# An encoder layer on eight cores: attention steps at whole instead of half yields, exponentials issued as a pair, new rates and stage order, and earlier loads

## Chip, cores, metric

One Trainium2 chip, all 8 cores, each with two of the 16 sequences. The metric is the device time of the slowest core in microseconds (us). Some executions fall in a slower state, in which one die, sometimes both, shows a lower granted TensorE clock (in a run of before of 4717.97 us, 0.817 to 0.821 on one die and 0.985 to 0.987 on the other); only fast runs are compared, or, where a chip was often disturbed, the mean span of the four cores of dies whose clock stayed above 0.978. That second measure ("die mean" below) lies some 10 to 25 us under the mean of the slowest core.

## The reference, cut

```python
x = x + 0.5 * swiglu(rmsnorm(x), gate1, up1, down1)          # feed-forward 1
h = rmsnorm(x); q_A,k_A,v_A,q_B,k_B,v_B,g = split(h @ w_in)
o_A = differential_attention(q_A,k_A,v_A)   # dense, 8 heads x 2 maps, ALiBi, per-head norm
o_B = window_attention(q_B,k_B,v_B,sink)    # |t-s| <= 128, 16 query and 4 key heads
x = x + (sig(g0)*(o_A @ P_A) + sig(g1)*(o_B @ P_B)) @ w_out
x = x + 0.5 * swiglu(rmsnorm(x), gate2, up2, down2)          # feed-forward 2
return rmsnorm(x)
# x: (16, 2048, 1024) float32; d_ff 2816
```

## The kernel before

A builder in Python emits all instructions in one order; semaphores follow from it. Each core has 8 blocks of 512 tokens. Stages are GU (gate and up of a feed-forward), D (down), W (input projections), P (gates and the two attention projections), O (output projection). Attention is not a stage: its 328 steps per sequence are put in between the dense products of other stages, so that TensorE has dense work while ScalarE (ACT) makes exponentials and VectorE (DVE) multiplies by the ALiBi table. Where steps may go in is a "yield" of a stage.

```python
def gemm8(self, b, bk, w, wk, H, hk):           # one PSUM bank of dense products
    for kc in range(8):
        self.mm(b, w[:, kc, :], H[:, kc, :], kc == 0, kc == 7, ...)
        if kc == 3:
            yield "h"                           # a half yield: a step may go in here
...
def b_qk(...):                                  # scores of one step: two PSUM pairs
    ...
    def ex(s, et, ek, W, tab, tk):
        self.act(et, scores, AF.Exp, ...)       # ACT, 128 x 1024
        self.tt(et, et, tab, ALU.mult, ...)     # DVE
    ex(*post[0])
    self.part.append(lambda: ex(*post[1]))      # emitted only at the next yield
...
def dole(self, n):                              # hands out queued DMA issues
    if self.dq[0]: ...                          # attention's loads first, by SyncE
    elif self.dq[1] and n - self.doled >= (3 if self.ph2 else 5): ...   # the rest
...
DENSE = {"GU": 0.22, "D": 0.40, "W": 0.34, "P": 0.28, "O": 0.22}  # attention per dense work
```

In the later part, loads and stores of the second kind are issued by POOL (GpSimd), which also computes the reciprocal roots of the attention's per-head norm (`rs`) and of the RMS norms. Weights come as float32, are cast to bf16 by POOL's transfers on first use, and are then read from a bf16 copy in memory.

The softmax here doesn't subtract the row's maximum and nothing guards it: scores larger than these inputs give would overflow.

## Time and profile before

| | before |
|---|---|
| median of the first 4 runs | 4113.34 us (4105.45 to 4573.34, the highest one slow) |
| slowest core in the profile | 4117.7 us |
| TensorE busy | 3931.4 us, 95% |
| DVE, ACT, POOL busy | 57%, 45%, 6% |

An engine's line of the page gives busy us, share of the span and the number of instructions. A timeline line gives start, duration, engine, line, operation, output<-inputs, count, and in brackets the idle time before it with what ended it. L376 is the helper that emits every matrix product, so products are told apart by their tiles: `H,ra` are dense ones of GU and W (normalized block, weights), `aT,rd` those of D, `qD,kD` dense-attention scores, `vD,et` their value products, `qS,kS` and `vS,es` the windowed ones. Of the tiles that products wait for, `et`, `es` and `est` are exponentials, `fr` the first pass over a dense bank, `sq` and `ssv` copies of projections on their way to memory, `nh` and `rh` steps of a norm, `obs` and `otS` attention outputs, `ra` and `rd` weights.

### The profile page before, as it was taken

How to read it: one execution, taken by the hardware profiler on the slowest of the kernel's cores; microseconds unless marked ns; L12 is line 12 of the kernel's file. 1: busy time of each engine (PE TensorE's matmuls, PEld its weight loads, DVE VectorE, ACT ScalarE, POOL GpSimd, SP SyncE). 2: the span in 40 equal slices, each digit the busy share in tenths (PEclk: the TensorE clock that was granted, in tenths of full speed). 3: DMA queues.
4: the chain of work that ended last, by engine and by line, in shares of the span. 5: the costliest groups of instructions: out<-in, count | busy, mean ns of one | idle time of the engine just before them, and what ended most of it. 6: DMA issues, size and time to landing. Idle time of an engine off the chain costs nothing.

```text
span 4117.7 us, 76905 instructions; the slowest of 8 cores (4074.8 to 4117.7 us)
## 1 busy us (share of the span) xinstructions
PE 3931.4 (95%) x27236; PEld 2026.8 (49%) x27236; DVE 2351.7 (57%) x4564; ACT 1863.1 (45%) x2576; POOL 251.3 (6%) x362
## 2 busy tenths in 40 slices
PE   8999998999998899999988999999998999999998
PEld 3444455555555455555544555555554544444443
DVE  5445232567677567666455667767767654353533
ACT  3422022656566466556455656656655532021211
POOL 1010000000001000000000000000000000000000
PEclk8999999999999999999999999999999999999999
DMA  8867599865678767755744544544544356465544
GB/s 186 201 135 184 134 205 182 188 165 147 152 179 190 196 157 184 188 149 160 218 125 140 154 129 145 166 132 139 158 135 146 113 172 219 154 194 168 185 153 130
DMA packets 296259, 675.25 MB, mean 164 GB/s; under 512 B 31280, under 2 KB 145328, under 8 KB 295216
## 3 DMA queue, kind: packets, MB, share of 16 engines
q1 hardware_dynamic: 263440, 542.65, 44.4%
q0 software_dynamic: 31872, 126.63, 16.4%
q8 instruction: 230, 3.77, 0.4%
q14 instruction: 141, 1.16, 0.1%
q10 hardware_dynamic: 576, 1.05, 0.1%
HBM read 605.09 MB, written 160.79 MB: 186 GB/s over the span
## 4 chain that ended last, share of the span: by engine, by line
PE 85%; DVE 4%; DMA 3%; issue 3%; ACT 2%; SPq 1%; POOL 0%; DVEq 0%; ACTq 0%; POOLq 0%
PE bank L376 85%; SPq L404 1%; ACT et L379 1%; PE bank L1133 1%; DVE nacc L382 1%; DMA vS<-vs_d 1%; DMA rd<-s_d 1%; DMA qs_d<-sq 1%; DVE et L382 0%; DVE H L385 0%; DMA oTa<-od_d 0%; ACT fr L379 0%; POOL r L382 0%; DMA ra<-s_win 0%; DMA H<-h_d 0%
## 5 line engine op out<-in xcount | busy, mean ns | idle before, releaser
L376 PE MATMUL bank<-H,ra 128*128 128x512 bf16 x8320 | 1915.5, 383 | 42.5 <-DMA H<-h_d 20.0
L376 PEld LDWEIGHTS bank<-H,ra 128*128 128x128 bf16 x8320 | 785.8, 98 | 1098.3 <-issue 258.2
L379 ACT ACTIVATE et<-bank 128x1024 bf16<-128x1024 f32 x1024 | 1011.2, 1022 | 443.2 <-PE bank L376 439.3
L382 DVE TENSOR_TENSOR et<-et,td 128x1024 bf16<-128x1024 bf16 x1024 | 701.8, 688 | 471.8 <-ACT et L379 470.3
L376 PE MATMUL bank<-aT,rd 128*128 128x512 bf16 x2816 | 643.4, 381 | 2.6 <-DMA rd<-s_d 1.6
L385 DVE SCALAR_TENSOR_TENSOR fr<-fr,bank 128x512 f32<-128x512 f32 x480 | 329.3, 686 | 441.5 <-ACT fr L379 354.6
L376 PE MATMUL bank<-vD,et 128*128 128x129 bf16 x8192 | 554.1, 221 | 18.8 <-DVE obs L382 17.1
L376 PEld LDWEIGHTS bank<-vD,et 128*128 128x128 bf16 x8192 | 503.7, 98 | 117.7 <-issue 37.4
L379 ACT ACTIVATE fr<-bank 128x512 f32<-128x512 f32 x352 | 210.1, 597 | 668.8 <-PE bank L376 659.8
L376 PEld LDWEIGHTS bank<-aT,rd 128*128 128x128 bf16 x2816 | 261.4, 98 | 358.2 <-issue 74.2
L376 PE MATMUL bank<-qD,kD 64*128 64x512 bf16 x2048 | 322.4, 384 | 18.2 <-ACT et L379 14.6
L385 DVE SCALAR_TENSOR_TENSOR R<-bank,R 128x512 f32<-128x512 f32 x192 | 132.2, 688 | 266.3 <-PE bank L376 266.0
L382 DVE TENSOR_TENSOR aT<-fr,bank 128x512 bf16<-128x512 f32 x352 | 240.6, 684 | 60.8 <-PE bank L376 58.5
L379 ACT ACTIVATE es<-bank 128x768 bf16<-128x768 f32 (+1 forms) x256 | 191.3, 781 | 141.2 <-PE bank L376 141.1
L379 ACT ACTIVATE fr<-bank,bgh 128x512 f32<-128x512 f32 x128 | 88.0, 687 | 301.7 <-PE bank L376 300.2
L382 DVE TENSOR_TENSOR es<-es,sw 128x768 bf16<-128x768 bf16 (+1 forms) x256 | 137.5, 539 | 131.1 <-ACT es L379 126.1
L382 POOL TENSOR_TENSOR rs<-ms,mhalf 128x4 f32<-128x4 f32 x64 | 74.4, 1163 | 2118.9 <-DVE ms L385 2118.9
L382 DVE TENSOR_TENSOR nacc<-nacc,ntmp 128x512 f32<-128x512 f32 x224 | 154.0, 688 | 55.5 <-ACT ntmp L379 50.6
L379 ACT ACTIVATE sq<-bank 128x512 bf16<-128x512 f32 x104 | 62.1, 597 | 259.3 <-PE bank L376 199.6
L379 ACT ACTIVATE ntmp<-R 128x512 f32<-128x512 f32 x224 | 133.9, 628 | 98.3 <-DVE nacc L382 55.9
L376 PE MATMUL bank<-ra,H 128*128 128x256 bf16 x1280 | 155.1, 278 | 12.9 <-ACT sq L379 11.6
L376 PEld LDWEIGHTS bank<-ra,H 128*128 128x128 bf16 x1280 | 123.7, 100 | 47.7 <-issue 29.0
(103 smaller groups left out, 2222.7 us busy)
## 6 DMA issues: line engine op xcount, KB each, us to landing
ra<-s_gu SPq DMA_DIRECT2D x275, 512.0 KB, 4.0
rd<-s_d SPq DMA_DIRECT2D x200, 352.0 KB, 3.2
ra<-s_win SPq DMA_DIRECT2D x81, 512.0 KB, 6.5
ra<-s_pg SPq DMA_DIRECT2D x64, 512.0 KB, 4.2
ra<-s_pp SPq DMA_DIRECT2D x64, 512.0 KB, 3.5
ra<-w_gu POOLq DMA_DIRECT2D x33, 512.0 KB, 7.2
qD<-qd_d SPq DMA_DIRECT2D x128, 128.0 KB, 4.5
R<-x_d POOLq DMA_DIRECT2D x32, 512.0 KB, 8.4
```

The costliest lines, as they stand in the source:

```text
L376: self.S.add("pe", lambda e: e.matmul(out, lhsT=lhsT, rhs=rhs, start=start, stop=stop), r=r, w=w)
L379: self.S.add("act", lambda e: e.activation(out=out, in_=in_, func=func, **kw), r=r, w=w)
L382: self.S.add(eng, lambda e: e.tensor_tensor(out=out, in0=a, in1=b, op=op), r=r, w=w)
L385: self.S.add("dve", lambda e: e.scalar_tensor_tensor(out=out, in0=a, scalar=s, in1=b, op0=op0, op1=op1), r=r, w=w)
L404: self.S.add(eng, lambda e: e.dma_start(out=out, in_=in_), r=r, w=w, dma=sem)
L1133: self.S.add("pe", lambda e, q=q: e.transpose(out=bt[:, q * 128:(q + 1) * 128], in_=src[:, q, :], identity=self.ident), r=[sk, "ident"], w ...
```

## The change

Its intent, as far as the diff tells: keep TensorE from waiting. Parts: no half yields; both exponentials of a step at once, only the second multiply put off; other rates; blocks 4 and 5 share one W stage and norms move; odd projection weights are cast ahead; windowed values (vS) loaded in halves; loads handed out faster, in the last W stage by SyncE; one drain of background work less. In the code, `bulk` means that POOL issues the loads of the second kind.

```diff
     def gemm8(self, b, bk, w, wk, H, hk):
         for kc in range(8):
             self.mm(...)
-            if kc == 3:
-                yield "h"
...
+        self.casts = [("win", i) for i in WORDER if i % 2]
+                if k == "D" and bl == (2, 3) and n % 7 == 0:
+                    self.cast()
...
-        elif self.dq[1] and n - self.doled >= (3 if self.ph2 else 5):
+        elif self.dq[1] and n - self.doled >= (1 if self.ph2 else 3 if self.w7 else 5):
...
         def ex(s, et, ek, W, tab, tk):
             self.act(... AF.Exp ...)
+        def al(s, et, ek, W, tab, tk):
             self.tt(... ALU.mult ...)
         ex(*post[0])
-        self.part.append(lambda: ex(*post[1]))
+        al(*post[0])
+        ex(*post[1])
+        self.part.append(lambda: al(*post[1]))
...
-            if bt == 7 and u < 7 and u % 2:
-                self.load_vS(sq, (u + 1) // 2)
+            if bt in (4, 7) and u < 7 and u % 2:
+                self.load_vS(sq, (u + 1) // 2, int(bt == 7))
...
-              ("GU", (4,), 1), ("D", (4,), 1), ("GU", (5,), 1), ("D", (5,), 1), ("W", (4,), 1)]
-        for b in (6, 7):
-            st += [("GU", (b,), 1), ("D", (b,), 1), ("W", (b - 1,), 1)]
-        st += [("W", (7,), 1)]
+              ("GU", (4,), 1), ("D", (4,), 1), ("GU", (5,), 1), ("D", (5,), 1), ("W", (4, 5), 1),
+              ("GU", (6,), 1), ("D", (6,), 1), ("GU", (7,), 1), ("D", (7,), 1), ("W", (6,), 1), ("W", (7,), 1)]
...
-        span = [(at("W", (2, 3), 1) + 32, w7 + 12), (w7 + 22, at("P", (4,), 2) - 6)]
+        span = [(at("W", (2, 3), 1) + 32, w7 + 4), (w7 + 22, at("P", (4,), 2) - 6)]
+            self.w7 = k == "W" and bl == (7,)
+            self.bulk = (ph == 2 or bl[0] >= 4) and not self.w7
...
-    DENSE = {"GU": 0.22, "D": 0.40, "W": 0.34, "P": 0.28, "O": 0.22}
+    DENSE = {"GU": 0.25, "D": 0.33, "W": 0.30, "P": 0.28, "O": 0.25}
...
         if k == "GU":
-            self.drain()
+            if b != 3:
+                self.drain()
... (where norms are started in the first part: cut)
```

More of the change, by code (lines that the diff above doesn't have):

```diff
@@ L295, in decl_chip @@
             S.region(("kSb", k), *S.regions[("kS", k)][:1], 2048, ("kS", k))
-        self.vS = sb("vS", [128, 16, 65], BF16)
+        self.vS = sb("vS", [128, 16, 65], BF16, keys=([("vS", k) for k in range(2)], 1040))
         self.sw = sb("sw", [128, 2, 384], BF16)
@@ L429, in init_rings @@
         self.ncast = 0
-        self.casts = [t for c in range(8) for t in (("pg", c), ("pp", c))] + [("wo", i) for i in range(4)]
+        self.casts = [("win", i) for i in WORDER if i % 2]
+        self.casts += [t for c in range(8) for t in (("pg", c), ("pp", c))] + [("wo", i) for i in range(4)]
         self.casts += [("gu2", f) for f in range(22)] + [("d2", c) for c in range(16)]
@@ L682, in gu_tile @@
         bg, bgk = self.bank(True)
-        yield from self.gemm8(bg, bgk, w[:, 0], wk, H, ("H", hi))
+        self.gemm8(bg, bgk, w[:, 0], wk, H, ("H", hi))
         t, tk = self.frn()
@@ L689, in gu_tile @@
         bu, buk = self.bank(True)
-        yield from self.gemm8(bu, buk, w[:, 1], wk, H, ("H", hi))
+        self.gemm8(bu, buk, w[:, 1], wk, H, ("H", hi))
         self.tt(self.aT[ai][:, f, :], s, bu, ALU.mult, [sk, buk], [("aT", ai, f)])
@@ L746, in w_tile @@
                                 tt == 0 and kc == 0, tt == 1 and kc == 7, [wk, ("H", hi, kc)], [bk])
-                    if tt == 0:
-                        yield "h"
                 self.open = None
@@ L773, in w_tile @@
                 bb, bk = self.bank(True)
-                yield from self.gemm8(bb, bk, w[:, j], wk, H, ("H", hi))
+                self.gemm8(bb, bk, w[:, j], wk, H, ("H", hi))
                 self.copy(("act", "dve")[j], st[:, j, :], bb, [bk], [("sq", q, j)])
@@ L788, in w_tile, with st_W @@
         yield
-    def st_W(self, bl, his, tiles):
-        for i in tiles:
-            w, wk = self.take("a")
-            for b, hi in zip(bl, his):
-                yield from self.w_tile(i, w, wk, b, hi)
-            self.issue("a")
+    def st_W(self, bl, his, lead=1):
+        held = {}
+        n = len(bl)
+        order = [(i, f) for i in range(n) for f in range(lead)]
+        order += [(i, f) for f in range(lead, len(WORDER)) for i in range(n)]
+        for i, f in order:
+            if i == 0:
+                held[f] = self.take("a")
+            yield from self.w_tile(WORDER[f], *held[f], bl[i], his[i])
+            if i == n - 1:
+                self.issue("a")
     def st_P(self):
@@ L806, in st_P @@
                 bb, bk = self.bank(True)
-                yield from self.gemm8(bb, bk, wg[:, s], wgk, H, ("H", 1))
+                self.gemm8(bb, bk, wg[:, s], wgk, H, ("H", 1))
                 t, tk = self.frn()
@@ L812, in st_P @@
                 src, nm = ((self.oTa, "oTa"), (self.oTb, "oTb"))[s]
-                yield from self.gemm8(bb, bk, wp[:, s], wpk, src, (nm,))
+                self.gemm8(bb, bk, wp[:, s], wpk, src, (nm,))
                 m, mk = self.frn()
@@ L830, in st_O @@
                 bb, bk = self.bank(True)
-                yield from self.gemm8(bb, bk, w[:, j], wk, self.mT, ("mT",))
+                self.gemm8(bb, bk, w[:, j], wk, self.mT, ("mT",))
                 self.stt(self.R[ri][:, c, :], bb, 0.5, self.R[ri][:, c, :], ALU.mult, ALU.add,
@@ L881, in load_sw, with load_vS @@
         self.later_dma("sw", self.sw, self.sw_d[p].rearrange("p (a b) -> p a b", a=2), [("swd", p)], ["sw"], ("bsw", 0), q=0)
-    def load_vS(self, sq, g):
-        self.later_dma("vS", self.vS, self.vs_d[sq, g], [("vs", sq, b) for b in range(4 * sq, 4 * sq + 4)], ["vS"], ("bvs", 0), q=0)
+    def load_vS(self, sq, g, k):
+        self.later_dma(("vS", k), self.vS[:, 8 * k:8 * k + 8, :], self.vs_d[sq, g][:, 8 * k:8 * k + 8, :],
+                       [("vs", sq, b) for b in range(4 * sq + 2 * k, 4 * sq + 2 * k + 2)], [("vS", k)], ("bvs", k), q=0)
     def first_loads(self, sq, part):
@@ L899, in first_loads @@
             self.load_sw(0)
-            self.load_vS(sq, 0)
+            self.load_vS(sq, 0, 0)
+            self.load_vS(sq, 0, 1)
             self.load_qD(sq, 0, 1)
@@ L916, in attention @@
             self.second()
-            if not self.half:
-                self.turn(i)
+            self.turn(i)
             if sq == 0 and i % 5 == 3:
@@ L922, in attention @@
                 self.b_av(i, i - LAG, batches[i - LAG], sq)
-            if self.half:
-                self.turn(i)
             if i < n:
@@ L1047, in b_av @@
         else:
-            self.flush("vS")
+            self.flush(("vS", 0))
+            if bt >= 4:
+                self.flush(("vS", 1))
             ns = [0] if bt == 0 else [2 * bt - 1, 2 * bt]
@@ L1055, in b_av @@
                     self.mm(self.bk[bank][:, o:o + 65], self.es_[x % 4][:, c_, col:col + 128], self.vS[:, x, :],
-                            z == 0, z == len(mm) - 1, [("est", x % 4), "vS"], [("bk", bank)])
+                            z == 0, z == len(mm) - 1, [("est", x % 4), ("vS", x // 8)], [("bk", bank)])
                 self.evac_S(i, sq, u, ns, bank)
-            if bt == 7 and u < 7 and u % 2:
-                self.load_vS(sq, (u + 1) // 2)
+            if bt in (4, 7) and u < 7 and u % 2:
+                self.load_vS(sq, (u + 1) // 2, int(bt == 7))
     def evac_D(self, i, sq, u, qb):
@@ L1182, in build @@
         self.slot = -1
-        self.half = False
+        self.urgent = False
         self.dc = 0
@@ L1187, in build @@
         self.ph2 = False
+        self.w7 = False
         self.load_x(0, True)
@@ L1209, in build @@
         for q, (a, b) in enumerate(span):
-            marks[a - (16, 10)[q]] = lambda q=q: self.first_loads(q, 0)
-            marks[a - (8, 6)[q]] = lambda q=q: self.first_loads(q, 1)
+            marks[a - (16, 14)[q]] = lambda q=q: self.first_loads(q, 0)
+            marks[a - (8, 8)[q]] = lambda q=q: self.first_loads(q, 1)
         n, done = 0, 0
@@ L1214, in build @@
             self.ph2 = ph == 2
-            self.bulk = ph == 2 or len(bl) == 1
+            self.w7 = k == "W" and bl == (7,)
+            self.bulk = (ph == 2 or bl[0] >= 4) and not self.w7
             self.gset = [6, 7] if any(a <= n < b for a, b in span) else [6, 7, 0, 1, 2, 3, 4, 5]
             self.rate = 3 if n == 0 else 1
-            for y in self.begin(k, bl, ph):
-                self.half = y == "h"
-                if not self.half:
-                    n += 1
-                    if n == 9:
-                        self.rate = 1
-                    if n in (40, 46, 52, 58):
-                        self.issue("d")
-                    if n in marks:
-                        while self.bg2:
-                            self.step()
-                        marks[n]()
-                    self.second()
-                    self.fill()
+            for _ in self.begin(k, bl, ph):
+                n += 1
+                if n == 9:
+                    self.rate = 1
+                if n in (40, 46, 52, 58):
+                    self.issue("d")
+                if k == "D" and bl == (2, 3) and n % 7 == 0:
+                    self.cast()
+                if n in marks:
+                    while self.bg2:
+                        self.step()
+                    marks[n]()
+                self.second()
+                self.fill()
+                self.post()
+                if self.urgent:
@@ L1232, in build @@
                     self.post()
-                    if k == "W" and len(bl) == 1 and n % 2:
-                        self.post()
-                    self.dole(n)
-                pos = cum[n] + (cum[n + 1] - cum[n]) / 2 if self.half else cum[n]
+                self.dole(n)
                 want = 0
                 for q, (a, b) in enumerate(span):
-                    if n >= a and pos > cum[a]:
-                        want = total * q + int(total * min(1.0, (pos - cum[a]) / (cum[b] - cum[a])) + 1e-6)
+                    if n > a:
+                        want = total * q + int(total * min(1.0, (cum[n] - cum[a]) / (cum[b] - cum[a])) + 1e-6)
@@ L1241, in build @@
                     if n == a:
                         self.gset = [6, 7]
-                if self.half and self.mark == "pe":
-                    continue
-                if done < want or len(self.gset) > 2 and not self.half:
+                if done < want or len(self.gset) > 2:
                     self.pre()
@@ L1251, in build @@
                 for q, (a, b) in enumerate(span):
-                    if n == b and not self.half:
+                    if n == b:
                         assert done == total * (q + 1)
@@ L1271, in begin @@
         b = bl[0]
-        two = len(bl) == 2
-        if ph == 1:
-            if two:
-                if k == "GU":
-                    if b == 0:
-                        self.load_x(2)
-                        self.load_x(3)
-                        return self.st_GU((0, 1), 4)
-                    self.drain()
-                    for j in range(2):
-                        self.store_x1(j)
-                        self.bg.append(self.norm(j, 1, j, store=lambda j=j: self.after2(j, j)))
-                    return self.st_GU((2, 3))
-                self.drain()
-                if k == "D":
-                    if b == 0:
-                        for j in (2, 3):
-                            self.bg.append(self.norm(j, 0, j, need=("x", j)))
-                    return self.st_D(bl)
+        if k == "D":
+            self.dc = 0
+            self.free = True
@@ new lines, in begin @@
+        if ph == 1 and b < 4:
+            if k == "GU":
+                if b == 0:
+                    self.load_x(2)
+                    self.load_x(3)
+                    return self.st_GU((0, 1), 4)
+                self.drain()
+                for j in range(2):
+                    self.store_x1(j)
+                    self.bg.append(self.norm(j, 1, j, store=lambda j=j: self.after2(j, j)))
+                return self.st_GU((2, 3))
+            self.drain()
+            if k == "D":
@@ L1291, in begin @@
                 if b == 0:
                     for j in (2, 3):
-                        self.store_x1(j)
-                        self.bg.append(self.norm(j, 1, j, store=lambda j=j: self.store_h2(j, j)))
-                else:
-                    self.bg.append(self.norm(0, 0, 0, need=("x", 4)))
-                self.S.add("dve", lambda e: e.memset(self.ssv[1], 1.0), w=[("ssv", 1)])
-                return self.st_W(bl, bl, WORDER)
+                        self.bg.append(self.norm(j, 0, j, need=("x", j)))
@@ L1299, in begin @@
+                return self.st_D(bl)
+            self.S.add("dve", lambda e: e.memset(self.ssv[1], 1.0), w=[("ssv", 1)])
+            if b == 0:
+                for j in (2, 3):
+                    self.store_x1(j)
+                    self.bg.append(self.norm(j, 1, j, store=lambda j=j: self.store_h2(j, j)))
+            else:
+                self.bg.append(self.norm(0, 0, 0, need=("x", 4)))
+            return self.st_W(bl, bl)
+        if ph == 1:
             if k == "GU":
                 self.drain()
+                if b in (5, 7):
+                    self.mix(b - 1)
@@ L1301, in begin @@
                 return self.st_GU((0,))
             if k == "D":
-                if b == 4:
-                    self.bg.append(self.norm(1, 0, 0, need=("x", 5)))
-                if b == 5:
-                    self.mix(4)
+                if b in (4, 6):
+                    self.bg.append(self.norm(1, 0, 0, need=("x", b + 1)))
+                else:
+                    self.mix(b, lambda c: self.dc > c)
                 return self.st_D(bl)
-            self.drain()
-            if b < 7:
-                self.mix(b + 1)
@@ L1311, in begin @@
-            if b < 6:
-                self.bg.append(self.norm(b % 2, 0, 0, need=("x", b + 2)))
+            if b == 4:
+                self.store_x1(5)
+                self.urgent = True
+                self.bg.append(self.norm(0, 0, 0, need=("x", 6)))
+                return self.st_W(bl, (1, 2), 4)
+            if b == 6:
+                self.store_x1(7)
             if b == 7:
+                self.drain()
                 self.load_p(0, (0,))
-            return self.st_W(bl, (self.MIX[b],), WORDER)
+            return self.st_W(bl, (self.MIX[b],))
@@ L1324, in begin @@
         if k == "GU":
-            self.drain()
+            if b != 3:
+                self.drain()
             if b == 2:
@@ L1333, in begin @@
             return self.st_GU((0,) if b < 7 else (1,))
-        self.dc = 0
-        self.free = True
         if b == 7:
@@ L1356, in end, with mix @@
                 self.bg.append(self.normf(5))
-    def mix(self, b):
-        self.store_x1(b)
-        self.bg.append(self.norm(b % 2, 1, self.MIX[b], store=lambda: self.after2(b, self.MIX[b])))
+    def mix(self, b, ready=None):
+        if ready is None:
+            self.store_x1(b)
+        self.bg.append(self.norm(b % 2, 1, self.MIX[b], store=lambda: self.after2(b, self.MIX[b]), ready=ready))
     def after2(self, b, hi):
         self.store_h2(b, hi)
+        self.urgent = False
         if b < 2:
```

## The prediction

> **What bounds the kernel now.** I read the busy shares first, then the stretches by stage, then TensorE's idle times one by one, and last the queues that ended them. The page and the stretches (PE first, then weight loads, DVE, ACT, POOL, granted clock, DMA share, GB/s):
>
> ```profile
> PE 3931.4 (95%) x27236; PEld 2026.8 (49%) x27236; DVE 2351.7 (57%) x4564; ACT 1863.1 (45%) x2576; POOL 251.3 (6%) x362
> PE 85%; DVE 4%; DMA 3%; issue 3%; ACT 2%; SPq 1%; POOL 0%; DVEq 0%; ACTq 0%; POOLq 0%
> ```
> ```profile
> 0.00:507.00 507.00, 485.00 (x2244) 217.11 (x2245) 215.99 (x348) 129.37 (x235) 42.75 (x77) 0.97 0.73 167
> 507.00:712.00 205.00, 188.62 (x1105) 107.15 (x1103) 71.90 (x115) 45.28 (x79) 13.30 (x22) 0.95 0.96 194
> 712.00:2075.00 1363.00, 1294.83 (x10693) 722.86 (x10693) 874.30 (x1815) 799.75 (x1053) 99.56 (x142) 0.99 0.69 175
> 2075.00:3346.00 1271.00, 1212.57 (x9659) 640.06 (x9658) 857.89 (x1773) 745.81 (x973) 65.69 (x79) 0.99 0.46 140
> 3346.00:4117.00 771.00, 750.41 (x3540) 339.58 (x3537) 331.63 (x514) 142.84 (x236) 29.99 (x42) 0.98 0.55 174
> ```
> TensorE bounds everything; no other engine is over 68% in any stretch. DMA is near its limit only at 507 to 712, the first input projections (stage W). So a change of order can win only what TensorE loses: 186 us idle (4117.7 − 3931.4), plus what it runs at a lower clock. Taking each product's undisturbed start-to-start time in this trace (0.2155 us at 512 columns, 0.056 us for an attention-value product), my sum over all products is about 3,685 us, which leaves some 420. Much of that is fixed. Each of the 656 attention steps costs about 0.2 us in switching between score products and others, 130 us in all; start and tail cost 40; neither is touched.
>
> (Program and trace both have 27,236 products; matched in order, they give each stage's times: first W 507 to 644, attention of sequence 0 from 712 to about 2010, of sequence 1 from about 2040 to 3340. A yield is the point after a bank of dense products at which the builder may put in an attention step: one batch of score products, exponentials, multiplies, and the value products of the batch two before.)
>
> The large idle times, in the timeline of TensorE (in brackets: idle before, and what ended it):
>
> ```profile
> 712.14 5.28 PE L376 MATMUL bank<-ra,H 128*128 128x256 bf16 x24 [11.59 <-ACT sq L379]
> 1386.08 0.38 PE L376 MATMUL bank<-vS,es 128*128 128x65 bf16 x4 [11.27 <-DMA vS<-vs_d]
> 2083.92 1.44 PE L376 MATMUL bank<-H,ra 128*128 128x512 bf16 x3 [7.79 <-DMA H<-h_d]
> 2211.24 1.86 PE L376 MATMUL bank<-H,ra 128*128 128x512 bf16 x4 [9.85 <-DMA H<-h_d]
> 2215.48 1.86 PE L376 MATMUL bank<-H,ra 128*128 128x512 bf16 x4 [2.38 <-DMA H<-h_d]
> 3162.12 0.16 PE L376 MATMUL bank<-onesb,nh 128*128 128x1 bf16 x1 [9.08 <-DVE nh L397]
> ```
> They stand on all cores that I looked at, within a few us of these sizes. The queues behind the second and third pair (SyncE's, then POOL's):
>
> ```profile
> 692.84 12.76 SPq L404 DMA_DIRECT2D vD<-vd_d  x3
> ```
> ```profile
> 2076.22 1.54 POOL L382 TENSOR_TENSOR rs<-ms,mhalf 128x4 f32<-128x4 f32 x1 [77.81 <-DVE ms L385]
> 2077.73 0.59 POOL L404 DMA_DIRECT2D oTb<-os_d  x1
> 2078.32 0.54 POOL L404 DMA_DIRECT2D H<-h_d  x1
> 2205.07 1.01 POOL L382 TENSOR_TENSOR rs<-ms,mhalf 128x4 f32<-128x4 f32 x1 [39.95 <-DVE ms L385]
> 2206.03 0.59 POOL L404 DMA_DIRECT2D H<-h_d  x1
> ```
> SyncE stood 12.8 us over three loads while transfers were saturated, and the store that frees a staging buffer sat behind it. POOL waited for an attention reciprocal root, and only then issued the gate stage's loads, although their buffers had been free for longer.
>
> [...] in the 12 us after the five stalls the granted clock was 0.76, 0.83, 0.76, 0.81 and 0.80. [...] The trace's projection weights cast into SBUF land in 9.6 us (median), plain ones in 6.5.
>
> **The change part by part.**
>
> 1. *Nine odd projection weights are cast ahead*, during the second down stage (431 to 507 us, TensorE losing nothing there, DMA share 0.63 in 400 to 500). The first W stage then has 9 fewer casts on POOL, the second 9 fewer casts and 9 fewer 512 KB stores out of SBUF. It targets the 712 us stall: 11.6 idle plus 0.24 × 12 = 2.9 of clock, 14.5 us. I give it 85%: 12.3.
> 2. *The windowed values vS come in two halves*, the first requested when window batch 4 of the old pair is done, not batch 7. An attention step takes about 4 us, so the half has some 20 steps instead of 5 steps (20 us, against the transfer's 25 us here). It targets 1386 us: 11.3 + 0.17 × 12 = 13.3; 95%: 12.6.
> 3. *In the last W stage, loads go by SyncE at a shorter spacing, and attention of sequence 0 ends 8 yields earlier.* The P loads start before POOL's root. Target 2084 us: 7.8 + 2.9 = 10.7; 80%: 8.6.
> 4. *The rates.* Working the progress formula by hand, at the start of the second P stage steps 0 to 40 of sequence 1 are emitted, against 0 to 41 before. The root of that head is emitted at step 41, so P's loads now stand ahead of it in POOL's queue and can go as soon as the preceding P ends, about 27 us earlier (2179, not 2206). The spacing of 1 instead of 3 does less: the attention loads of a new head go first. Target 2211: 9.85 + 2.38 + 0.19 × 12 = 14.5; 70%: 10.2.
> 5. *No drain before the third feed-forward of the last part.* The final norm of the block before then runs behind products. Target 3162: 9.1, with 0.6, 1.8 and 0.9 of its next three waits, 12.5, + 0.20 × 12 = 14.9; 90%: 13.4.
> 6. *Norms move from W stages into feed-forward stages, and blocks 4 and 5 share W.* Three norm waits (4.6 at 568, 2.8 at 1242, 3.8 at 1879 us) and their clock, about 17 us; half: 8. Weight waits, 5.6: 2.
> 7. *Exponentials issued as a pair, only the second multiply put off.* Frees the score banks sooner. TensorE waits 15.3 us for these in 838 to 3346; half: 8.
> 8. *Half yields go.* Steps can come only every 8 dense products: 1.72 us of those and 1.35 plus 0.2 us of attention, 3.3 us, against two exponentials at 1.02 and some 0.3 to 0.6 of dense work on ACT (2.6), and two multiplies at 0.69 plus 0.7 and 0.5 on DVE (2.6). It fits, with little room. Feed-forward takes about 30 steps instead of 25 or 27, W 0.83 a yield instead of 0.86 to 0.89. I charge 7 us for new short waits, the casts' contention with the down weights included.
>
> The instruction work stays the same, except the saved weight loads and moved casts. Sum: 12.3 + 12.6 + 8.6 + 10.2 + 13.4 + 8 + 2 + 8 − 7 = 68 us. 4113 − 68 = 4045 us, 1.7% faster.
>
> **The rivals.** *The finer interleave was worth more than I think.* Then many waits of 0.2 to 1 us replace five long ones. For it: DVE is at 65 to 75% under attention, and the denser feed-forward raises that. Against it: down stages have no half yields before either, run 0.72 to 0.75 steps per 1.2 us yield, and lose little. 0.1 us per step is 66 us, and the gain is gone: about 4110. *The stalls move.* POOL's queue still orders roots and loads, and a spacing of 1 fills it with loads that wait for output stores (14 waits, 91.7 us already)[...]. Half of the gain stays: about 4080. *The clock and the small waits gain more*: all five stalls go fully (68), norm and bank waits too (40): about 4005.
>
> **Range and chances.** The five stalls are measured and their causes visible, so slower needs the first rival in full, and more. 2% is 82 us, above my sum but below what all targets together would give. Time 4045, range 3995 to 4092; faster by over 2%: 0.37, within: 0.59, slower: 0.04.
>
> **What would show it.** Right: no TensorE idle over 5 us between 60 and 4000 us, clock 1.00 in those stretches, busy near 97%; H loads issued ahead of the root at the second P. Wrong: a new long wait for down weights at 431 to 507, for H of block 5 at the shared W, or for POOL roots; or, with the stalls gone, more idle spread over the feed-forward stages ended by ACT and DVE, which would mean step 8 was undercharged.

Its clock terms (0.24 × 12 and the like) are estimates from the granted clocks measured in the 12 us after each stall, 0.76 to 0.83. In the trace of before the clock goes to 0.50 at about 704, 1380, 2080, 2206 and 3158 us, inside the five idle times, and stays there for 10 to 14 us; in 838 to 952 us, where TensorE is busy for 113.9 of 114 us, it is 1.00. Where SyncE stood 12.8 us, the DMA share was 0.98 (692 to 706 us), and the store `qs_d<-sq` behind it went at 705.75. The rival "the stalls move" loses its last link, from a late root to TensorE: DVE waited for one twice, 2.6 us in all, and a wait of TensorE after that was not shown.

## The result, and the profile after

The changed kernel took 4024.5 us (median of 10 runs, 4018.26 to 4275.37); before, over all its 15 runs of that comparison, 4129.58. The ratio is 0.9776, 95% interval 0.9758 to 0.9795: 2.2% faster. Ratios here are the mean time of one kernel's fast runs over that of the other's in the same rounds, so not quite the ratio of the medians. The prediction was 4045 with 4113 for before, 1.7%. The time lies inside the range, but the likeliest class was "within 2%" (0.59) and the result is just beyond it (0.37 was given).

The page's line and the stretches after, cut at the corresponding stage boundaries (columns as in the prediction):

```profile
PE 3909.6 (97%) x27236; PEld 2015.7 (50%) x27236; DVE 2350.3 (58%) x4564; ACT 1865.6 (46%) x2576; POOL 244.7 (6%) x345
```
```profile
0.00:515.00 515.00, 488.62 (x2246) 217.93 (x2247) 215.97 (x349) 128.57 (x235) 47.22 (x86) 0.96 0.78 172
515.00:703.00 188.00, 185.15 (x1103) 105.87 (x1101) 71.89 (x115) 45.31 (x79) 6.95 (x10) 0.98 0.91 219
703.00:2025.00 1322.00, 1279.12 (x10659) 715.36 (x10660) 868.39 (x1803) 798.40 (x1051) 95.11 (x132) 0.99 0.70 170
2025.00:3258.00 1233.00, 1200.95 (x9694) 635.78 (x9693) 862.06 (x1786) 750.50 (x977) 65.44 (x75) 1.00 0.50 144
3258.00:4036.00 778.00, 755.80 (x3539) 340.79 (x3536) 332.00 (x514) 142.86 (x236) 29.97 (x42) 0.97 0.54 173
```
The first stretch is 8 us longer, the next three (first input projections, then attention of the two sequences under the dense stages) are 17, 41 and 38 us shorter, the last is 7 us longer (its clock is 0.97, not 0.98). Idle TensorE time fell from 186 to 126 us; the rest of the 82 us on the slowest core is in how fast it ran (3909.6 us busy instead of 3931.4, at a mean granted clock of 0.987 instead of 0.981).

TensorE's longest idle times that are left (timeline of the changed kernel, start and end of the program left out):

```profile
508.36 3.83 PE L376 MATMUL bank<-aT,rd 128*128 128x512 bf16 x10 [3.93 <-DMA rd<-w_d]
...
703.33 2.88 PE L376 MATMUL bank<-ra,H 128*128 128x256 bf16 x13 [2.83 <-ACT sq L379]
...
1277.94 0.27 PE L376 MATMUL bank<-ident,rh 128*128 128x128 bf16 x1 [6.41 <-ACT ssv L379]
...
1973.16 13.48 PE L376 MATMUL bank<-H,ra 128*128 128x512 bf16 x48 [4.64 <-DMA ra<-s_win]
...
3251.45 4.00 PE L376 MATMUL bank<-aT,rd 128*128 128x512 bf16 x9 [5.33 <-DMA rd<-s_d]
```
None of the five stalls of before is there in its old size: that at 712 shrank from 11.6 to 2.8 us, the others are gone. The wait at 508 us for down weights is the price of the casts that were moved there (DMA share 0.86 in 431 to 515 us, before 0.53 in 431 to 507; gone in kernel 9, which makes them earlier); that at 1278 is new. So one sign that the prediction named, no idle time over 5 us between 60 and 4000 us, was not met: 6.4 and 5.3 us are left. And POOL's queue around the second P, which now starts at 2140 us:

```profile
2113.79 0.60 POOL L404 DMA_DIRECT2D H<-h_d  x1 [3.64 <-PE bank L376]
...
2117.47 0.53 POOL L404 DMA_DIRECT2D H<-h_d  x1
...
2148.13 1.38 POOL L382 TENSOR_TENSOR rs<-ms,mhalf 128x4 f32<-128x4 f32 x1 [29.09 <-DVE ms L385]
```
The loads of H go 26 us ahead of their use, and the root stands behind them.

To see the small waits too, I added up, product by product, how much later the next one started than it does undisturbed (mean of the 6 cores whose records are complete; "long" are over 2.5 us, "small" 0.12 to 2.5, with what ended them; score to dense switches are in "small"):

| us | before | after |
|---|---|---|
| all | 400 | 310 |
| long | 75 | 31 |
| of these: H / vS / sq / norm (nh) | 24 / 11 / 10 / 24 | 0 / 0 / 4 / 12 |
| of these: weights (ra, rd) | 3 | 10 |
| small | 302 | 248 |
| of these: for exponentials (et, est) | 40 | 0.3 |
| for attention outputs (obs, otS) | 31 | 56 |

So the long waits gave 44 us, and the small ones 54, of which the waits for exponentials alone gave 40. The prediction gave these 8. How large they come out depends on what counts as undisturbed: where the next pair of score products is allowed the 0.22 us that it takes after a pair when nothing holds it up, the 40 are some 30. They come in some 50 pieces.

### The profile page after: what moved, and what is told of

Read it like the earlier page. It is cut to its first block, busy times and chain, and to the rows that moved or that the text cites. A ratio compares the mean times of both kernels' runs of the same rounds, so it can differ in the third digit from the quotient of the medians.

```text
span 4035.8 us, 77085 instructions; the slowest of 8 cores (3999.9 to 4035.8 us)
## 1 busy us (share of the span) xinstructions
PE 3909.6 (97%) x27236; PEld 2015.7 (50%) x27236; DVE 2350.3 (58%) x4564; ACT 1865.6 (46%) x2576; POOL 244.7 (6%) x345
## 4 chain that ended last, share of the span: by engine, by line
PE 88%; DVE 4%; DMA 3%; issue 2%; SPq 1%; ACT 1%; POOL 0%; DVEq 0%; ACTq 0%; POOLq 0%
PE bank L376 88%; SPq L404 1%; PE bank L1140 1%; DVE et L382 0%; DMA oTa<-od_d 0%; DMA rd<-w_d 0%; DVE H L385 0%; DVE obs L382 0%; DVE osq L382 0%; DMA ra<-s_win 0%; DVE R L385 0%; POOL r L382 0%; DMA R<-x 0%; DMA rd<-s_d 0%; DVE nacc L382 0%
## 5 line engine op out<-in xcount | busy, mean ns | idle before, releaser
L379 ACT ACTIVATE et<-bank 128x1024 bf16<-128x1024 f32 x1024 | 992.5, 1022 | 431.6 <-PE bank L376 426.6
L376 PE MATMUL bank<-qD,kD 64*128 64x512 bf16 x2048 | 310.2, 381 | 0.0
L385 DVE SCALAR_TENSOR_TENSOR H<-R,gains,nrb 128x512 bf16<-128x512 f32 x192 | 138.6, 745 | 6.7 <-ACT nrb L379 6.7
```

Source lines behind the costliest of these rows:

```text
L376: self.S.add("pe", lambda e: e.matmul(out, lhsT=lhsT, rhs=rhs, start=start, stop=stop), r=r, w=w)
L379: self.S.add("act", lambda e: e.activation(out=out, in_=in_, func=func, **kw), r=r, w=w)
L385: self.S.add("dve", lambda e: e.scalar_tensor_tensor(out=out, in0=a, scalar=s, in1=b, op0=op0, op1=op1), r=r, w=w)
```

## The experiments

The question was then which part is worth what: theory A, that the stalls are the gain; rival B, that interleave matters; C, that small waits do; D, that stalls only move. Each ratio is against the kernel before on the same chip; die means are given in the same way. Most differences are under 2%; their intervals still show what is clear of noise.

### 1. Half yields out, nothing else

```diff
-            if kc == 3:
-                yield "h"
-                    if tt == 0:
-                        yield "h"
```

> The kernel before with the half yields alone taken out (attention steps only between whole banks of dense products; order, rates, loads and exponentials as before). Theory A, that the gain is the long stalls: the finer interleave is worth little, so this is 0 to 15 us slower than before (ratio 1.000 to 1.004), and the waits of score products for exponentials grow from 18 us to perhaps 30. Rival B, that the interleave is worth 0.1 us a step or more: 40 to 70 us slower (1.010 to 1.017).

Measured: 1.0048 (1.0019 to 1.0077), 20 us slower; die mean 4122.5 against 4103.8. The groups of dense-attention score products, before and in this kernel (busy, mean ns of one | idle time before them, and what ended it):

```profile
L376 PE MATMUL bank<-qD,kD 64*128 64x512 bf16 x2048 | 322.4, 384 | 18.2 <-ACT et L379 14.6 <-ACT es L379 1.8
```
```profile
L376 PE MATMUL bank<-qD,kD 64*128 64x512 bf16 x2048 | 330.1, 383 | 51.3 <-ACT et L379 44.3 <-ACT es L379 5.1
```
The waits grew from 18 to 51 us, more than I expected. With all small ones counted (as in the table above) they went from 40 to some 100, while the waits for H fell from 24 to 9, which hid part of it. The timeline of a W stage of this kernel shows how a wait arises:

```profile
1620.21 1.02 ACT L379 ACTIVATE et<-bank 128x1024 bf16<-128x1024 f32 x1 [2.01 <-PE bank L376]
...
1620.25 1.90 PE L376 MATMUL bank<-H,ra 128*128 128x512 bf16 x8
...
1621.99 1.08 PE L376 MATMUL bank<-vD,et 128*128 128x129 bf16 x16
...
1622.31 0.60 ACT L379 ACTIVATE sq<-bank 128x512 bf16<-128x512 f32 x1 [1.07 <-PE bank L376]
...
1622.80 1.02 ACT L379 ACTIVATE et<-bank 128x1024 bf16<-128x1024 f32 x1
...
1623.96 0.39 PE L376 MATMUL bank<-qD,kD 64*128 64x512 bf16 x2 [0.57 <-ACT et L379]
```
After its first exponential, ACT stands still for 1.07 us, because the next thing in its queue is the copy of a dense bank that is not finished. The second exponential, whose scores have long been ready, comes after that copy. It ends at 1623.8, and the scores that need its bank have been waiting.

### 2. Exponentials as a pair, half yields kept

```diff
+        def al(s, et, ek, W, tab, tk):
             self.tt(... ALU.mult ...)
         ex(*post[0])
-        self.part.append(lambda: ex(*post[1]))
+        al(*post[0])
+        ex(*post[1])
+        self.part.append(lambda: al(*post[1]))
```

> The kernel before with both exponentials of a step issued at once and only the second multiply put off, half yields kept. Theory A as in the prediction's step 7: the 18 us that score products wait for exponentials go, half of it shows: 8 to 15 us faster (ratio 0.996 to 0.998). Rival C, that the small waits were the larger part of the gain: 25 us or more faster (0.994 or less). If the order of exponentials does nothing: 1.000.

Measured: 0.9928 (0.9895 to 0.9961), 30 us faster; die mean 4073.8 against 4103.8. That is rival C's number. Waits for exponentials are gone; but some of TensorE's waits are now for DVE's first pass over dense banks. Two lines of the waits in this kernel (waiter <- releaser: us, times, longest):

```profile
PE bank L376 <- DVE fr L385: 11.2, 18, 0.9
...
PE bank L1137 <- DVE fr L385: 6.9, 12, 0.8
```
In before they were 1.0 and 1.9 us. A step put in at a half yield leaves 4 dense products, 0.86 us, before the dense bank's own ACT work, which now stands behind two exponentials of 1.02 us.

### 3. Both together

The two diffs above, on the kernel before.

> The two together on the kernel before: no half yields, exponentials as a pair. If the pair is what makes whole yields affordable, this is as fast as the pair alone (0.996 to 1.000) although the first kernel of this series is slower. Rival B: 30 us or more slower than before (1.007 or more).

Measured: 0.9798 (0.9771 to 0.9826), 83 us faster; die mean 4023.7. Alone the two parts make −30 and +20 us; together −83. This one kernel, without any of the parts that aim at the stalls, has nine tenths of the change's gain. I had expected at most the gain of the pair. The same place in the program, in this kernel's timeline:

```profile
1585.21 1.94 ACT L379 ACTIVATE et<-bank 128x1024 bf16<-128x1024 f32 x2 [1.87 <-PE bank L376]
...
1585.25 1.90 PE L376 MATMUL bank<-H,ra 128*128 128x512 bf16 x8
...
1586.99 1.08 PE L376 MATMUL bank<-vD,et 128*128 128x129 bf16 x16
...
1587.30 0.60 ACT L379 ACTIVATE sq<-bank 128x512 bf16<-128x512 f32 x1 [0.16 <-PE bank L376]
...
1588.00 0.61 PE L376 MATMUL bank<-qD,kD 64*128 64x512 bf16 x4
```
ACT makes both exponentials (1.94 us together) under the 8 dense products (1.90 us together) and is free, with 0.16 us to spare, when the dense bank is done; all four score products then run without a break. Relative to the pair alone, taking the half yields out removed 17 us of waits for H, 23 of waits for `fr`, and 6 for vS.

### 4. Three local parts on the kernel before

vS in halves, no drain before the third feed-forward, casts ahead (the lines of the diff above).

> The kernel before with three local parts of the change: vS in halves, no drain before the third feed-forward, odd projection weights cast ahead. Interleave, rates, order and exponentials as before. Theory A: the stalls near 712, 1386 and 3162 us go, 11.6 + 11.3 + 12.5 idle and about 7 of clock, with the probabilities of the prediction about 38 us (ratio 0.991, between 0.989 and 0.993). Rival D, stalls only move: under 15 us (over 0.996). The stalls at 2084 and 2211 us for H stay as they are.

Measured: 0.9918 (0.9886 to 0.9950), 34 us; die mean 4074.5. As theory A has it. vS waits went from 10.8 to 0, the sq stall from 9.5 to 3.3, norm waits from 23.8 to 14.4; new: 3.3 us for down weights and 2.9 for weights of gate and up (`ra<-s_gu`). By stage, the two first W stages lost 8 us less than in before and the down stage that now holds the casts 6 more, so here the casts are worth some 2 us, and most of the 34 is from vS and the drain.

### 5. The changed kernel with the old rates

```diff
-    DENSE = {"GU": 0.25, "D": 0.33, "W": 0.30, "P": 0.28, "O": 0.25}
+    DENSE = {"GU": 0.22, "D": 0.40, "W": 0.34, "P": 0.28, "O": 0.22}
```

> The changed kernel with the rates of before (feed-forward 0.22, down 0.40, W 0.34, gate 0.28, output 0.22). The prediction's step 4 said that the rates are what puts the second P's loads ahead of the attention root in POOL's queue: if so, TensorE waits 10 us or more for H at the start of the second P again, and the time rises by 10 to 20 us (ratio to before about 0.981). The kernel before without half yields lost that stall with its rates unchanged (8.8 us of H waits in all instead of 24.0), so the rival is that the half yield put the root there: then no H wait over 3 us, and the time stays within 8 us (0.976 to 0.979).

Measured: 0.9783, interval 0.9696 to 0.9869 because the chip was often disturbed; die mean 4001.6 against 4100.0, ratio 0.976. No core waits for H at the first or second P; the longest such wait anywhere is 1.6 us, at 3351. In the changed kernel, the new rates are worth nothing that I could measure; this run supports the rival named there, not my step 4 as a whole (see 12).

### 6. The changed kernel without the pair

```diff
         ex(*post[0])
         al(*post[0])
-        ex(*post[1])
-        self.part.append(lambda: al(*post[1]))
+
+        def both():
+            ex(*post[1])
+            al(*post[1])
+
+        self.part.append(both)
```

> The changed kernel with the second exponential put off again together with its multiply. Without half yields the deferral costs much: the kernel before had 40 us of TensorE waits for exponentials, 100 without half yields, 5 with the pair and no half yields. Expected: waits for exponentials 60 to 100 us, time 60 to 90 us up (ratio to before 0.991 to 1.000), so the change without this one part would have gained little. Had the stalls been the gain (the prediction's theory), it would rise by about 8 us (0.979 to 0.981).

Only one of its 8 runs was fast. On the undisturbed dies the mean was 4123.1 (8 dies) against 4100.0 for before: slower than before, and some 115 us above the changed kernel's 4007 to 4009. A core in which the clock was 0.991 has among its waits:

```profile
PE bank L376 <- ACT et L379: 73.6, 100, 1.4
```
More than I expected (60 to 90 us), and the clearest single result: by this measure the change without this part would have been a loss of 23 us. It rests on die means.

### 7. The changed kernel with three stalls put back

vS asked for only after window batch 7, the drain back, the last W stage's loads by POOL at the old spacing.

> The changed kernel with three local parts undone: vS asked for in both halves only after window batch 7, the drain before the third feed-forward of the last part, and the last W stage's loads by POOL at the old spacing. If the stalls add up simply: 11 + 12 + 8 idle and 5 to 7 of clock come back, 30 to 40 us (ratio 0.985 to 0.988). If a stall only moves, under 15 us (under 0.982).

Measured: 0.9807 (0.9747 to 0.9866); die mean 4033.8 (ratio 0.984) against 0.9775 for the changed kernel (10), so 25 us come back, somewhat less than the 30 to 40 expected. The interval of the ratio alone would not tell the two apart. Two of its waits:

```profile
PE bank L376 <- DMA ra<-s_win: 21.5, 6, 13.1
...
PE bank L376 <- DMA vS<-vs_d: 10.3, 1, 10.3
```
vS is back with 10.3 us, and norm waits rose from 12 to 21. But without the last W stage's rule TensorE does not wait for H at the first P, as it did in before (7.8 us); it waits for projection weights, 13.1 us at once, at 1972 us in that last W stage (4.6 us there in the changed kernel). There the stall moved, as rival D has it; that this rule and not one of the other two parts brings it back is inferred from the place.

### 8. Pair, whole yields and the three local parts, in before's order

The diffs of 1, 2 and 4 together.

> A candidate to beat both: the kernel before without half yields, with the exponentials as a pair, and with vS in halves, no drain, casts ahead; its order of stages, norms and rates stay. If these parts add up, 0.9798 with another 34 us off: ratio 0.970 to 0.973, about 4005 us, and the shared W stage, the moved norms and the new rates of the change are worth nothing or less than nothing. If they are worth what the prediction gave them (norms 8, weights 2): not under 0.978.

Measured: 0.9772 (0.9697 to 0.9847); die mean 4002.8 against 4100.0, 0.976. The parts do not quite add up: by die means 80 and 29 alone, 97 together. H at the first P still costs it 9 us. It equals the changed kernel without that one's order of stages, moved norms, rates and quicker loads.

### 9. A version to beat both

```diff
+        elif self.dq[1] and n - self.doled >= (1 if self.ph2 else 3 if self.w7 else 5):
...
+            self.w7 = k == "W" and bl == (7,)
+            self.bulk = (ph == 2 or len(bl) == 1) and not self.w7
...
+                    if k == "GU" and bl == (2, 3) and n % 9 == 0:
+                        self.cast()
```
on top of kernel 8 (new lines only; the last two, casts earlier, replace those for stage D).

> A version meant to beat both: bf_three (before's order and rates, no half yields, exponentials as a pair, vS in halves, no drain, casts ahead) with the last W stage's loads by SyncE at the shorter spacing, and the nine casts spread over the second feed-forward instead of the second down stage. What was left in bf_three: 9 us of waits for H at the first P, 4 to 5 us for down weights at 450 to 505 us, 3 us at 700, each with its clock. Expected 8 to 18 us under bf_three, whose ratio of undisturbed dies was 0.976: 0.972 to 0.974, 5 to 20 us under the changed kernel on the same chip. If the loads only move into another wait: equal to bf_three.

Measured: 0.9723 (0.9702 to 0.9744), the mean of its fast runs 3999.2 us; die mean 3990.5, 12 us under kernel 8 by the ratios. It beats the changed kernel on the same chip (0.9784, die mean 4007.3) by 17 us. H waits are 1.3 us, the down-weight waits of 450 to 505 gone; the sq stall stays (5.3), so its reason is not the casts alone. A wait for weights of gate and up, of which before has none, stays as well (7.6 us in two pieces). Waits for attention outputs are 41 us, as in kernels 3 and 8; the changed kernel has 56.

```profile
PE 3885.5 (97%) x27236; PEld 2012.4 (50%) x27236; DVE 2349.7 (59%) x4564; ACT 1866.2 (47%) x2576; POOL 240.6 (6%) x345
```

### 10. The changed kernel again

> The changed kernel itself, unedited, on the same chip as the others of this series, so that they can be compared without a second chip between. Expected as on record: ratio 0.9776 (0.976 to 0.979).

Measured: 0.9784 (0.9749 to 0.9820), die mean 4007.3. As expected.

### 11. The changed kernel with half yields put back

The `yield "h"` lines and the half positions of the main loop as in before; the pair stays.

> The changed kernel with the half yields put back, the pair of exponentials kept. From the two kernels on before (pair with half yields 0.9928, without 0.9798) half yields cost 53 us once the pair is there: then this is 30 to 55 us slower than the changed kernel (0.985 to 0.991), the waits of dense banks for VectorE (the fr tiles) grow from 1 to some 15 to 25 us. The prediction's step 8 had it the other way: half yields back would win up to 7 us (0.976).

Its result was wrong (relative error 0.030). All instructions run, so some product must read a tile in the wrong order; I did not find which, and the time counts with that reserve. 0.981 (0.9786 to 0.9834), die mean 4020.2, 13 us above the changed kernel, not 30 to 55. The waits for `fr` did grow, from 2 to 19 us, as expected; those for attention outputs (obs, otS) fell from 56 to 30. So half yields with the pair cost 53 us in before's order and rates, where they brought the H stalls with them, and little here. My expectation took over a number from another context.

### 12. The new rates on the kernel before

> The kernel before with the rates of the change alone, half yields and deferral kept. Worked from the progress formula, the root of step 41 is then emitted after the second P's loads although half yields stay: the wait for H at the start of the second P goes (24 us of H waits in all to about 10) and the time falls by 10 to 20 us (0.995 to 0.998), so rates and missing half yields each suffice for that stall. If H stays at 20 us or more, the step's reason was wrong and only the half yields count.

Measured: 0.9900 (0.9883 to 0.9917), 41 us faster, far more than expected; die mean 4059.5 against 4099.7. POOL around the second P (which starts at about 2177 us):

```profile
2146.38 1.01 POOL L382 TENSOR_TENSOR rs<-ms,mhalf 128x4 f32<-128x4 f32 x1 [36.87 <-DVE ms L385]
2151.07 0.59 POOL L404 DMA_DIRECT2D H<-h_d  x1 [3.69 <-PE bank L376]
...
2154.76 0.53 POOL L404 DMA_DIRECT2D H<-h_d  x1
...
2184.78 1.38 POOL L382 TENSOR_TENSOR rs<-ms,mhalf 128x4 f32<-128x4 f32 x1 [28.45 <-DVE ms L385]
```
The loads stand ahead of the root, and H waits fell from 24.0 to some 1 us, at the first P as well. So the rates suffice for both stalls, and missing half yields suffice for the second. By stage, with the usual switches between kinds of products taken out, losses in P, O, D and W fell by 16, 9, 10 and 7 us, in GU not at all. H accounts for P and O. Why D and W lose less was not traced; with the new rates a D stage of the second part takes 20 attention steps instead of 24, and a GU stage 30 instead of 26 or 27. Waits for exponentials did not fall (`et` alone: 35 to 34).

## Why the prediction was right or wrong, point by point

**What bounds the kernel: right.** TensorE's instructions and their number stayed; what changed is how long TensorE waits.

**Step 1, casts ahead (12 us): right in kind, much less.** The stall fell by 6 to 9 us, but the down stage before, as "wrong" had listed, lost 6 us more. In the changed kernel the two first W stages lost 14 us less, but without any casts ahead kernel 3 has 6 of these; with the local parts alone (4) they lost 8 less, some 2 net. Made in the feed-forward instead (9), the casts cost the down stage nothing.

**Step 2, vS in halves (13): right.** 10.8 to 0; undoing it brings 10.3 back.

**Step 3, last W stage (9): the stall went, the reason was incomplete.** Experiment 7 suggests, by the place of the wait, that what the rule prevents in the changed kernel is a 13 us wait for weights; the wait for H is also removed by the rates alone.

**Step 4, rates (10): the mechanism was right, and not the only one.** The rates do put the loads ahead of the root (12), missing half yields do as well (1, 3), and with the latter the rates add nothing (5). Counting them as a separate gain was a mistake in the accounting. Alone, they are worth four times the 10 us, of which the waits for H explain 23; the rest stays open.

**Step 5, the drain (13): right.** The wait at 3162 us is gone; undoing it with two others brings 9 us of norm waits back.

**Step 6, norms and shared W (10): not borne out.** One norm wait of 6.4 us appeared at 1278 for three that went, weight waits did not fall, and before's order did as well (8) and better (9). What the order alone is worth was not run.

**Step 7, the pair (8): the mechanism was right, its size was not.** This is the failed term. I read 15.3 us in the table of waits and took half. Alone it made 30 us (2), and in the changed kernel its absence costs some 115 (6). The table of waits missed part: summed over all products the waits for exponentials were 30 to 40 us, in some 50 pieces, most of them under a microsecond. And it left out what the pair makes possible, the next step.

**Step 8, whole yields (7 us lost): wrong in sign, given the pair.** My budget per step (2.6 us on ACT and on DVE under 3.3 us of products) was right, and the timeline in 3 shows it, but it holds only with the pair. I priced 7 and 8 as two independent terms. They are one: alone −30 and +20, together −83. The stalls alone would have given 34 (4) to some 45 us (the table).

**The rivals.** The first, that the finer interleave was worth more, is refuted: it was worth 20 us only with the second exponential put off. The second, stalls move, is true for one of them (7). The third, "the clock and the small waits gain more", came nearest: it said that norm and bank waits go too, though its 4005 is as far from the result as the 4045.

**The number was in part luck.** The sum of 68 us put 67 on stalls, norms and weights and 1 on the pair and the whole yields together. Measured, these two alone make 83, and all the rest of the change adds some 10 on top. The time came inside the range because terms that overlap were added up as if they were separate, and this nearly made up for the coupled pair that was missed. (Its "some 420" us of loss is 433 by its own figures; nothing rests on it.)

**What stays open.** Parts substitute for each other: the rates are worth 41 us on before and nothing in the changed kernel; the local parts 34 alone and about 17 on top of the pair and whole yields. I did not run every combination, so no share of the 92 us can be given to a part as its own.

## What to carry to other kernels

When two queues are interleaved, ask what stands in an engine's queue between two pieces of ready work: in experiment 1 an exponential whose scores were ready stood behind a copy that was not, and ACT stood still for 1.07 us. Price coupled parts of a change together, and sum many short waits over the whole trace before halving a number from a table of waits. A load that shares a queue with small arithmetic should be emitted before the arithmetic whose input is late: in before, POOL's loads of H stood behind a root of 1.01 us until 2206 us and TensorE waited 9.85 us for them; emitted ahead of the root, as in the changed kernel, they left 26 us before their use.

## What the traces show besides

- All eight cores ran dense products for 4 ms at a mean granted clock of 0.97 to 0.996 in fast runs. Means near 0.8 stand only in slow runs, such as the one of 4717.97 us. Short stretches at such a clock stand in a fast run too: in the profile of before, two cores of one die have six each at 0.812, 15 us long.
- In the trace of before a score product starts some 98 ns late after a value product (153 ns after it, where the next value product starts after 56), and a dense product 92 ns late after a score product (308 instead of 216); over 656 steps this makes an estimated 125 us of 4118.
- In the page of before POOL's queue moved 126.63 MB in 16.4% of the engines' time, SyncE's 542.65 MB in 44.4%: 1.6 times the time per byte (of the destination), with casts among them.
